# A decoder layer with a top-2 mixture of experts: one token table loaded whole, the late norms' passes moved apart, and two blocks' statistics on the scalar engine

## The chip, the cores and the metric

One core of one Trainium2 chip runs the whole program in one launch. The metric is the device time of that core in microseconds (us). The engines are TensorE (PE, with its weight loads as PEld), VectorE (DVE), ScalarE (ACT), GpSimd (POOL) and SyncE (SP); ACT, POOL and SP also issue DMAs, shown as ACTq, POOLq and SPq. Each engine runs its own instructions strictly in order.

## The reference, cut to what matters

One layer over 2048 tokens of width 1024. A mixer with attention and a recurrence comes first and is not touched. Then:

```
x = layer_norm(ALPHA * x + mix @ w_out, ln1_g, ln1_b)
scores = sigmoid(x @ w_router); sel = scores + router_bias      # 16 experts in 4 groups
best = argmax over groups of the sum of the two largest sel     # one group per token
idx  = the two experts of that group with the largest sel;  w = their scores, normalised
y[token] += w * (silu(x @ w_gate[e]) * (x @ w_up[e])) @ w_down[e]   # for its two experts
out = layer_norm(ALPHA * x + y, ln2_g, ln2_b)
```

## The kernel before, in words

Three stages follow each other: attention and recurrence to about 720 us, the out projection with router (`outproj_phase`) to about 940 us, and the experts (`moe_phase`) to the end. Tile pools make the dependences; a scheduler sets the order on DVE, ACT, POOL and SP by a simulated timeline, while PE keeps the written order. `issue_after` (through `after`) gives the scheduler an order, `hold` adds a real wait.

**Router.** For each of 16 blocks of 128 tokens `route_block` picks two experts per token on DVE, and `rank_block` gives each choice a rank within its expert and scatters the pair (token, weight) with a POOL DMA into row `expert * 2304 + rank` of table `T[j]`, one table for each of the two choices (L1238). Both tables are filled with a large number beforehand, so that the minimum of the two is the list of an expert's tokens.

**Hand-over.** `plan_slots` sorts the experts by count; slot s takes the s-th largest, with room for `CAPS[s]` tokens (336 down to 256). `fetch` reads the rows of slot 0's expert from both tables with two SP DMAs (L1499), takes the minimum and gathers the tokens' rows of x (`xg`, L1490) with three POOL DMAs. `fetch_all` reads the first 384 rows of all 16 experts from both tables with six ACT DMAs (L1515) and builds the lists of all slots on DVE (L1516 to L1529). PE multiplies dummy matrices (L77) from the moment that `early` (L1768) exists, then transposes the gathered tokens (L1542); ACT and DVE split each transposed tile into a high and a low part (L1544).

**One expert.** `gemm1` makes four pairs of products j = 0 to 3 (gate and up, L63), each of 24 matmuls per product over weights that were loaded (L1620) and split by ACT (L1628) and DVE (L1629). DVE multiplies silu(gate) by up (`sl`, L1639), ACT and DVE split the result (`h`, L1650 and L1651). Down weights are split by L1605 and L1606. `gemm2` (L1687) multiplies h with them, and between its steps PE transposes the next expert's tokens. The result is added to `zd` in memory by a POOL DMA (L1724). The weight loads of product j = 1 of slot 0 are held until slot 0's gather has landed.

**Norms.** The second layer norm is done block by block when all of a block's tokens are ready, by the table `READY`: slots 9, 11, 13 and 14 and 15 normalise two blocks each, slots 10 and 12 one. `scale` takes the statistics on DVE (L1571, L1573, L1580) and the root on POOL (L1581), `write` makes two passes of 1024 columns on DVE (L1585, L1586), and `put` scatters the rows to the output (L1591). Blocks for the next slot are fetched by `bring` (L1562). In slot 15 the last three fetched blocks and the two row tiles of its own result are normalised with `late=True`: there the root is taken on ACT as Ln and Exp (L1577, L1578).

Of the kernel before, what the change touches and what calls it, by code (L numbers as in the profile page):

```python
# [23 lines left out]
D = 1024  # L24
# [637 lines left out]
def hgrn_phase(c):  # L662

    nc, tc, a = c.nc, c.tc, c.a
    with ExitStack() as es:
# [239 lines left out]
        for g in range(NG + 1):  # L905
            if 2 <= g < 4:
                load = fill_tables(c, pad, g - 2)
                hold(c, load, c.level)
# [110 lines left out]
EROWS = 2304  # L1019
BIG = 4096.0  # L1020
NE = 16
CAPS = (336, 320, 304, 296, 288, 280, 280, 272, 264, 264, 256, 256, 256, 256, 256, 256)
# [3 lines left out]
def outproj_phase(c):  # L1026

    nc, tc, a = c.nc, c.tc, c.a
    with ExitStack() as es:
# [40 lines left out]
        c.idx = c.cp.tile([128, S // 128, 2], F32, name="idx")  # L1070

# [98 lines left out]
def route_block(c, sm, ps_r, pr, blk, rb, code, tok):  # L1170
# [11 lines left out]
    mxp, mnp = T([4, 2], "mxp"), T([4, 2], "mnp")  # L1182
    tt(mxp, sel[:, :, 0:2], sel[:, :, 2:4], OP.max)
    tt(mnp, sel[:, :, 0:2], sel[:, :, 2:4], OP.min)
    m1, m2, m3 = T([4], "m1"), T([4], "m2"), T([4], "m3")
    tt(m1, mxp[:, :, 0], mxp[:, :, 1], OP.max)
    tt(m2, mxp[:, :, 0], mxp[:, :, 1], OP.min)
    tt(m3, mnp[:, :, 0], mnp[:, :, 1], OP.max)
    tt(m2, m2, m3, OP.max)
    tt(m1, m1, m2, OP.add)  # L1190
    gm = T([1], "gm")
    v.tensor_reduce(out=gm, in_=m1, axis=AX.X, op=OP.max)
# [25 lines left out]
    return row, idx, oh, ohs  # L1218


def rank_block(c, sm, ps_r, tri, row, idx, oh, ohs):
# [14 lines left out]
    v.scalar_tensor_tensor(dst, idx, float(EROWS), rank, op0=OP.mult, op1=OP.add)  # L1236
    for j in range(2):
        nc.gpsimd.indirect_dma_start(out=c.T[j][:, :], out_offset=bass.IndirectOffsetOnAxis(ap=dst[:, j:j + 1], axis=0),  # L1238
                                     in_=row[:, j], in_offset=None)


def plan_slots(c, pl, ps):
# [9 lines left out]
    r.lt = T([NE, NE], "lt")  # L1252
# [122 lines left out]
def plan_over(c, pl, r, big):  # L1375
# [68 lines left out]
    v.scalar_tensor_tensor(orow, oe, float(EROWS), orow, op0=OP.mult, op1=OP.add)  # L1444
    yield
    c.orow = cp.tile([128, NOV], I32, name="orow")
    v.tensor_scalar(c.orow, orow, 0.0, float(NE * EROWS - 128), op0=OP.max, op1=OP.min)
# [3 lines left out]
def moe_phase(c):  # L1451
# [4 lines left out]
    with ExitStack() as es:  # L1456
# [37 lines left out]
        def fetch(row, C):  # L1494

            nch = (C + 127) // 128
            tab = sm.tile([128, 2, NCH, 2], F32, name="tab", bufs=2)[:, :, :nch]
            for j in range(2):
                nc.sync.dma_start(tab[:, j], c.T[j][ds(row, nch * 128), :].rearrange("(n p) w -> p n w", p=128))  # L1499
            tb = sm.tile([128, NCH, 2], F32, name="tb", bufs=2)[:, :nch]  # L1500
            v.tensor_tensor(out=tb, in0=tab[:, 0], in1=tab[:, 1], op=OP.min)
            ig = sm.tile([128, NCH], I32, name="ig", bufs=2)[:, :nch]
            v.tensor_scalar(ig, tb[:, :, 0], float(S - 1), None, op0=OP.min)
            io = sm.tile([128, NCH], I32, name="io", bufs=2)[:, :nch]
            v.tensor_copy(io, tb[:, :, 0])
            return gathered(dict(ig=lambda n: ig[:, n:n + 1], io=lambda n: io[:, n:n + 1], w2=lambda n: tb[:, n, 1:2]), C)

        def fetch_all(eos, big):

            both = [yp.tile([128, D], F32, name="zt", bufs=ZT)[:, :NE * NCH * 2].rearrange("p (e n w) -> p e n w", e=NE, w=2)  # L1510
                    for j in range(2)]
            for j in range(2):
# [96 lines left out]
        def gemm1(f, e, C, first=False, late=False, beside=lambda j: None):  # L1609
# [6 lines left out]
            for j in range(4):  # L1616
                ps = []
                for w in (wg, wu):
# [6 lines left out]
                    with ExitStack() as order:  # L1625
                        if j and first:
                            after(order, *f["last"])
# [133 lines left out]
        with tc.manual_schedule(engines={mybir.EngineType.PE}):  # L1761
# [12 lines left out]
            for s in range(NE):  # L1774
# [14 lines left out]
                with ExitStack() as order:  # L1789
# [6 lines left out]
                    else:  # L1796
                        after(order, f["mul"])
                        for _ in range(15):
                            next(over, None)
# [93 lines left out]
```

## Time and profile before

| what | before |
|---|---|
| median of three runs (lowest, highest) | 1678.7 us (1671.63, 1680.99) |
| the profiled execution, its span | 1675.53 us, 1674.0 us |
| busy PE, PEld, DVE, ACT, POOL | 1522.5, 1361.2, 1186.1, 816.8, 548.3 us |
| granted TensorE clock over the span | 0.969 |
| PE busy in 924 to 966 us and 966 to 1008 us | 14.31 and 30.58 of 42 us |
| PE busy in 1092 to 1386 us | 42.00 of each 42 us |

The span counts from the first to the last instruction; 1.5 us of the execution lie around it. A timeline row reads: start, duration, engine, line, operation, written tile <- read tiles, shapes, count, and in brackets how long the engine stood idle before it and for what. Rows with the same line and operation that follow closely are merged into one.

### The profile page before, as it was taken

The page shows a single profiled execution, that of the slowest core. Times are in us where ns is not written, and L with a number is a line of the kernel's source. Part 1 is how long each engine was busy: PE and PEld are TensorE (multiplying, and loading weights), DVE is VectorE, ACT ScalarE, POOL GpSimd, SP SyncE. Part 2 cuts the span into 40 slices and gives each one's busy share as a digit, 9 for nine tenths or more (in the row PEclk, how much of TensorE's full clock was granted, in tenths as well). Part 3 has the DMA queues.
Part 4 walks back from the last instruction along what each step waited for, and adds up shares of the span by engine and source line. Part 5 has one row for each costly group of instructions (what it writes and reads, how often), then busy time and mean ns, then how long its engine had stood idle before and what let it go on. Part 6 is the DMA issues. An engine that isn't in the chain of part 4 may idle for free. (4 is left out here: it accounts for less than half of the span.)

```text
span 1674.0 us, 28474 instructions
## 1 busy us (share of the span) xinstructions
PE 1522.5 (91%) x10293; PEld 1361.2 (81%) x10293; DVE 1186.1 (71%) x2780; ACT 816.8 (49%) x1824; POOL 548.3 (33%) x729
## 2 busy tenths in 40 slices
PE   8899999978898998899999379999999999999994
PEld 7899999877788887777777268988888888989883
DVE  5688888896977778777888454555555556666767
ACT  4566767676243343443342143555555555545443
POOL 3233333466644433322333211111111124232342
PEclk9999999999999999999999689999999999999997
DMA  9422222342222122263431587777777778888872
GB/s 273 154 95 89 96 96 96 121 145 75 64 64 65 58 63 60 80 233 129 175 139 77 123 225 212 195 196 199 189 202 198 204 223 247 251 246 258 248 220 100
DMA packets 241581, 258.67 MB, mean 155 GB/s; under 512 B 26224, under 2 KB 191249, under 8 KB 241436
## 3 DMA queue, kind: packets, MB, share of 16 engines
q1 hardware_dynamic: 203216, 182.03, 34.8%
q0 software_dynamic: 21088, 69.86, 15.5%
q10 hardware_dynamic: 17132, 4.91, 1.4%
q8 instruction: 83, 1.36, 0.3%
q14 instruction: 62, 0.51, 0.1%
HBM read 189.32 MB, written 69.01 MB: 154 GB/s over the span
## 5 line engine op out<-in xcount | busy, mean ns | idle before, releaser
L63 PE MATMUL ph<-xt,w 128*128 128x256 f32 (+8 forms) x3072 | 399.0, 291 | 5.7 <-DVE w L1629 5.7
L63 PEld LDWEIGHTS ph<-xt,w 128*128 128x128 f32 x3072 | 396.8, 189 | 8.8 <-DVE w L1629 7.0
L63 PE MATMUL pj<-xt,w 128*128 128x256 f32 x2016 | 290.4, 287 | 10.4 <-DVE xt L139 4.0
L63 PEld LDWEIGHTS pj<-xt,w 128*128 128x128 f32 x2016 | 259.3, 191 | 16.7 <-DVE xt L139 5.4
L1687 PE MATMUL py<-w,h 128*128 128x512 f32 (+8 forms) x936 | 243.3, 405 | 13.1 <-DVE h L1651 12.1
L1629 DVE TENSOR_TENSOR w<-raw,w 128x1024 fp32r<-128x1024 f32 x128 | 153.1, 1219 | 85.8 <-ACT w L1628 85.7
L1687 PEld LDWEIGHTS py<-w,h 128*128 128x128 f32 (+8 forms) x936 | 160.6, 179 | 58.4 <-DVE h L1651 14.7
L63 PE MATMUL py<-w,xt 128*128 128x512 f32 x672 | 174.5, 408 | 0.6 <-ACT xt L943 0.4
L1628 ACT ACTIVATE w<-raw 128x1024 fp32r<-128x1024 f32 x128 | 132.2, 1053 | 63.0 <-PE ph L63 42.5
L1724 POOL DMA_INDIRECT zd<-z,ioall x37 | 57.4, 1551 | 321.3 <-ACT xt L1544 213.7
L63 PEld LDWEIGHTS py<-w,xt 128*128 128x128 f32 x672 | 123.7, 192 | 29.0 <-issue 4.6
L1544 DVE TENSOR_TENSOR xt<-tr,xt 128x512 fp32r<-128x512 f32 (+8 forms) x84 | 50.2, 598 | 123.4 <-ACT xt L1544 123.3
L63 PE MATMUL pj<-w,xt 128*128 128x512 f32 x336 | 90.5, 409 | 0.0
L795 DVE TENSOR_TENSOR qb<-qq,F 64x256 f32<-64x256 f32 x112 | 83.1, 742 | 5.1 <-ACT F L769 2.0
L339 POOL TENSOR_SCALAR prob<-prob,den 128x128 f32<-128x128 f32 x128 | 46.2, 380 | 107.6 <-ACT prob L382 57.8
L813 DVE COPY_PREDICATED A<-mask,pl 128x512 f32<-128x512 uint8 x56 | 49.9, 891 | 40.4 <-PE pl L811 39.9
L1544 ACT ACTIVATE xt<-tr 128x512 fp32r<-128x512 f32 (+8 forms) x84 | 43.8, 521 | 70.7 <-PE tr L1542 70.5
L1634 ACT ACTIVATE sl<-ph 128x256 f32<-128x256 f32 (+8 forms) x64 | 25.7, 402 | 102.7 <-PE ph L63 102.6
L1606 DVE TENSOR_TENSOR w<-raw,w 128x2048 fp32r<-128x2048 f32 x32 | 73.1, 2284 | 0.0
L1238 POOL DMA_INDIRECT T<-row,dst x32 | 34.3, 1073 | 111.3 <-DVE dst L1236 95.2
L811 PEld LDWEIGHTS pl<-qb,kb 128*128 128x128 f32 x384 | 49.1, 195 | 26.4 <-POOL kb L799 12.7
L63 PEld LDWEIGHTS pj<-w,xt 128*128 128x128 f32 x336 | 61.6, 194 | 10.9
(387 smaller groups left out, 2864.1 us busy)
## 6 DMA issues: line engine op xcount, KB each, us to landing
raw<-in_w_gate SPq DMA_DIRECT2D x64, 512.0 KB, 5.1
raw<-in_w_up SPq DMA_DIRECT2D x64, 512.0 KB, 5.8
raw<-in_w_down SPq DMA_DIRECT2D x32, 1024.0 KB, 8.6
xd<-xt SPq DMA_DIRECT2D x32, 512.0 KB, 7.0
xr<-in_x SPq DMA_DIRECT2D x14, 1024.0 KB, 6.3
xt<-xd POOLq DMA_DIRECT2D x20, 512.0 KB, 4.8
raw<-mixT SPq DMA_DIRECT2D x16, 512.0 KB, 5.1
x1d<-x SPq DMA_DIRECT2D x16, 512.0 KB, 2.6
```

Source lines behind the costliest of these rows:

```text
L63: nc.tensor.matmul(ps, lhsT=a, rhs=b, start=i == 0, stop=i == len(steps) - 1)
L339: nc.gpsimd.tensor_scalar(prob[:, h], prob[:, h], den[:, h:h + 1], 1.0, op0=OP.mult, op1=OP.mult)
L795: nc.vector.tensor_tensor(out=qb[l][rw, :, :, o].rearrange("p a c (n i) -> p (a c) n i", i=h), in0=sec(Qv), in1=sec(Fv), op=OP.mult)
L811: nc.tensor.matmul(pl[:, ch, p], lhsT=kt[:, p, ch * 128:(ch + 1) * 128], rhs=qb[l][:, p, ch].rearrange("p o i -> p (o i)"), start=True, st ...
L813: c.level = nc.vector.copy_predicated(A.rearrange("p c h (n u i) -> p (c h n) u i", u=2, i=h)[:, :, 1], mask[:, l].rearrange("p m (n i) -> ...
L1238: nc.gpsimd.indirect_dma_start(out=c.T[j][:, :], out_offset=bass.IndirectOffsetOnAxis(ap=dst[:, j:j + 1], axis=0), in_=row[:, j], in_offse ...
L1544: f["last"] = nc.scalar.activation(hi, pt, AF.Copy), v.tensor_tensor(out=lo, in0=pt, in1=f32(hi), op=OP.subtract)
L1606: v.tensor_tensor(out=t[:, 1], in0=raw, in1=f32(t[:, 0]), op=OP.subtract)
L1628: nc.scalar.activation(t[:, 0], raw, AF.Copy)
L1629: v.tensor_tensor(out=t[:, 1], in0=raw, in1=f32(t[:, 0]), op=OP.subtract)
L1687: nc.tensor.matmul(pys[hf][:m], lhsT=lhs, rhs=rhs, start=k == 0 and i == 0, stop=k == 3 and i == len(steps[k]) - 1)
L1724: add = nc.gpsimd.indirect_dma_start(out=zv[n], out_offset=at, in_=z[:r], in_offset=None, bounds_check=S - 1, oob_is_err=False, compute_op ...
```

## The change

1. **One table.** `T[0]` and `T[1]` become one table `P`, laid out by rank: row `(rank % 128) * 272 + (rank // 128) * 16 + expert`, 272 being 17 chunks of 16 experts. Partition p then finds the first 384 ranks of all experts in 96 neighbouring numbers, and one ACT DMA loads them (L1524 of the new kernel). The row needs `rank // 128`, made by 16 comparisons and a sum (`table_row`), four DVE instructions instead of one. One fill instead of two; each scatter writes its own view of `P`.
2. **Lists in two parts.** `of_slots` builds the list of slot 0 alone from the loaded tile, and those of slots 1 to 15 after slot 0's transposes. `fetch` is left for the overflow loop, which doesn't run here.
3. **Group choice.** The sum of the two largest of four becomes the maximum over six pair sums: five DVE instructions instead of eight.
4. **Norms.** With two blocks in a slot, the first is written at product j = 1 and the second at j = 2 (both at j = 1 before). `bring` comes after the roots on POOL.
5. **Late blocks.** In slot 15 a table that has Ln and Exp is loaded once on ACT after the last silu; of the three late blocks the first keeps `scale`, the other two take their statistics on ACT (`sums_of`: a sum, a sum of squared differences, Ln, Exp).
6. `ln2_g` and `ln2_b` are loaded in the out projection (on ACT's queue) instead of in slot 0.

```diff
-    v.scalar_tensor_tensor(dst, idx, float(EROWS), rank, op0=OP.mult, op1=OP.add)
+    table_row(c, dst, rank, idx, ge, n, place, 2)
     for j in range(2):
-        nc.gpsimd.indirect_dma_start(out=c.T[j][:, :], out_offset=bass.IndirectOffsetOnAxis(ap=dst[:, j:j + 1], axis=0),
+        nc.gpsimd.indirect_dma_start(out=c.pv[2 * blk + j], out_offset=bass.IndirectOffsetOnAxis(ap=dst[:, j:j + 1], axis=0),
...
+def table_row(c, dst, rank, expert, ge, n, place, m):
+    v = c.nc.vector
+    v.tensor_tensor(out=ge, in0=rank[:, :, None].to_broadcast([128, m, NCK - 1]),
+                    in1=c.steps[:, None, :].to_broadcast([128, m, NCK - 1]), op=OP.is_ge)
+    v.scalar_tensor_tensor(place, rank, float(ROWS), expert, op0=OP.mult, op1=OP.add)
+    v.tensor_reduce(out=n, in_=ge, axis=AX.X, op=OP.add)
+    v.scalar_tensor_tensor(dst, n, float(NE - 128 * ROWS), place, op0=OP.mult, op1=OP.add)
...
-            for j in range(2):
-                rows = c.T[j].rearrange("(e r) w -> e r w", r=EROWS)[:, 0:NCH * 128].rearrange("e (n p) w -> p e n w", p=128)
-                for n in range(NCH):
-                    nc.scalar.dma_start(both[j][:, :, n], rows[:, :, n])
-            v.tensor_tensor(out=both[0], in0=both[0], in1=both[1], op=OP.min)
+            c.tabled = nc.scalar.dma_start(tab, c.P.rearrange("(p n e) w -> p n e w", p=128, n=NCK)[:, :NCH])
...
+        def sums_of(t, late):
+            z, junk = t["z"], w1p.tile([128, KC, 128], F32, name="raw1").rearrange("p k n -> p (k n)")
+            act, m = nc.scalar.activation, sm.tile([128, 4], F32, name="sums", bufs=2)
+            act(junk, z, AF.Identity, accum_out=m[:, 0:1])
+            act(m[:, 1:2], m[:, 0:1], AF.Copy, scale=-1.0 / D)
+            act(junk, z, AF.Square, bias=m[:, 1:2], accum_out=m[:, 2:3])
+            act(t["mv"][:, 0:1], m[:, 0:1], AF.Copy, scale=1.0 / D)
+            act(t["rs"], m[:, 2:3], AF.Ln, scale=1.0 / D, bias=eps2)
+            act(t["rs"], t["rs"], AF.Exp, scale=-0.5)
...
+            tab, hot = tables(r.eos)
+            slots = of_slots(tab, hot, 0, 1, big)
             f = start(0)
...
-                    if j == 1:
-                        for t in brought:
+                    if j in (1, 2):
+                        for t in brought[:1] if j == 1 else brought[1:]:
                             f["passed"] = write(t, t["z"])
...
                     if s == 0:
-                        slots = fetch_all(r.eos, big)
+                        after(order, *f["last"])
+                        slots = of_slots(tab, hot, 1, NE - 1, big)
                         nxt = start(1)
...
-                        after(order, f["low"])
+                        after(order, f["low"], f["silu"])
+                        nc.scalar.preload_act_table_set("natural_log_exp_and_others")
+                        for n, t in enumerate(brought):
+                            (sums_of if n else scale)(t, late=True)
```

PE's order is unchanged from the first instruction to the last. Three places move on the other engines.

On ACT at the hand-over, before. `zt<-T` are the six loads of `fetch_all`, `early` is what PE's dummy products wait for, `w` the split weights of slot 0's first two products, `xt` its transposed tokens:

```order
L1287 ACTIVATE eos<-py 128x16
L1515 DMA zt<-T_89 128x16x2 x3
L1515 DMA zt<-T_90 128x16x2 x2
L1768 ACTIVATE early<-tb 128x128
L1515 DMA zt<-T_90 128x16x2
L1628 ACTIVATE w_11542<-raw_11540 128x1024
L1628 ACTIVATE w_11572<-raw_11570 128x1024
L1544 ACTIVATE xt_11484<-tr 128x4x128 x2
```

The same place on ACT in the changed kernel (`tab` is the one load of `P`):

```order
L1299 ACTIVATE eos<-py 128x16
L1524 DMA tab<-P 128x96
L1655 ACTIVATE w_11581<-raw_11579 128x1024
L1655 ACTIVATE w_11611<-raw_11609 128x1024
L1797 ACTIVATE early<-tb_11484 128x128
L1558 ACTIVATE xt_11523<-tr 128x4x128 x2
```

Six loads became one, and `early` went behind the two weight casts. On DVE before, at the same place, the lists of all slots (L1516 to L1529) stood between the weights of slot 0 and its transposed tokens `xt`:

```order
L1629 TENSOR_TENSOR w_11572<-raw_11570,w_11572 128x1024
L1516 TENSOR_TENSOR zt<-zt 128x96
L1523 TENSOR_TENSOR zt<-zt,m 128x768 x2
L1525 TENSOR_REDUCE tball<-zt 128x48 x2
L1544 TENSOR_TENSOR xt_11484<-tr,xt_11484 128x4x128
L1527 TENSOR_SCALAR igall<-tball 128x48
L1529 CAST ioall<-tball 128x48
```

The same place on DVE now, from the second weight split on:

```order
L1656 TENSOR_TENSOR w_11611<-raw_11609,w_11611 128x1024
L1558 TENSOR_TENSOR xt_11523<-tr,xt_11523 128x4x128 x2
L1558 TENSOR_TENSOR xt_11523<-tr,xt_11523 128x4x80
L1558 TENSOR_TENSOR xt_11524<-tr,xt_11524 128x4x128 x2
L1558 TENSOR_TENSOR xt_11524<-tr,xt_11524 128x4x80
L1537 TENSOR_TENSOR zt<-tab,hot 128x720 x2
```

The lists of slots 1 to 15 (`128x720`) moved behind the tokens. On DVE in slot 14, from the first block's second pass (`zt<-zt,rs,b`) to `h` of product 2, before. Ahead of these rows stand `sl` of product 1, the first passes (two before, one now), a down split and two weight splits:

```order
L1586 SCALAR_TENSOR_TENSOR zt<-zt,rs,b_11383 128x1024
L1651 TENSOR_TENSOR h<-sl,h 128x256
L1586 SCALAR_TENSOR_TENSOR zt<-zt,rs,b_11383 128x1024
L1639 TENSOR_TENSOR sl<-sl,ph 128x256
L1606 TENSOR_TENSOR w_17829<-raw_17827,w_17829 128x2048
L1629 TENSOR_TENSOR w_18001<-raw_17999,w_18001 128x1024
L1629 TENSOR_TENSOR w_18031<-raw_18029,w_18031 128x1024
L1629 TENSOR_TENSOR w_18082<-raw_18080,w_18082 128x1024
L1651 TENSOR_TENSOR h<-sl,h 128x256
```

The same stretch of DVE now:

```order
L1613 SCALAR_TENSOR_TENSOR zt<-zt,rs,b_11416 128x1024
L1678 TENSOR_TENSOR h<-sl,h 128x256
L1666 TENSOR_TENSOR sl<-sl,ph 128x256
L1612 SCALAR_TENSOR_TENSOR zt<-zt,mv,g_11415 128x1024
L1633 TENSOR_TENSOR w_17864<-raw_17862,w_17864 128x2048
L1656 TENSOR_TENSOR w_18036<-raw_18034,w_18036 128x1024
L1656 TENSOR_TENSOR w_18066<-raw_18064,w_18066 128x1024
L1656 TENSOR_TENSOR w_18117<-raw_18115,w_18117 128x1024
L1613 SCALAR_TENSOR_TENSOR zt<-zt,rs,b_11416 128x1024
L1678 TENSOR_TENSOR h<-sl,h 128x256
```

The second block's two passes went behind the second `sl`; from `sl` of product 1 to `h` of product 2 both orders hold the same instructions. On ACT in slot 15 of the changed kernel, from the last silu on (before, the two `h` followed the silu at once, then five times a table load, Ln, a table load, Exp):

```order
L1661 ACTIVATE sl<-ph 128x256
L1840 ACT_TABLE_LOAD
L1601 ACTIVATE raw_18347,sums<-zt 128x1024
L1677 ACTIVATE h<-sl 128x256
L1601 ACTIVATE raw_18357,sums<-zt 128x1024
L1602 ACTIVATE sums<-sums 128x1 x2
L1603 ACTIVATE raw_18347,sums<-zt,sums 128x1024
L1603 ACTIVATE raw_18357,sums<-zt,sums 128x1024
L1677 ACTIVATE h<-sl 128x256
```

The table load and the four passes over two late blocks stand ahead of the last two `h`, or between them; the ten table loads are gone.

## Rows read from the trace of the kernel before

**Rows 1.** Busy time by stretch: stretch, its length, then PE, PEld, DVE, ACT, POOL busy us with counts, the granted TensorE clock, the DMA share and GB/s. The out projection, the hand-over, slot 0.
```profile
840.00:882.00 42.00, 42.00 (x242) 33.27 (x241) 36.55 (x145) 15.24 (x32) 14.76 (x14) 1.00 0.38 139
924.00:966.00 42.00, 14.31 (x97) 7.47 (x95) 18.63 (x105) 8.08 (x20) 10.46 (x11) 0.67 0.58 115
966.00:1008.00 42.00, 30.58 (x180) 29.34 (x181) 24.48 (x29) 17.34 (x21) 6.62 (x6) 0.86 0.77 221
```

**Rows 2.** The timeline of the hand-over, 941 to 964 us.
```profile
941.54 0.96 POOL L1238 DMA_INDIRECT T<-row,dst  x1 [0.30 <-issue]
...
943.15 1.29 SPq L1499 DMA_DIRECT2D tab<-T  x2
943.15 15.42 ACTq L1515 DMA_DIRECT2D zt<-T  x5
944.67 0.37 SPq L1620 DMA_DIRECT2D raw<-in_w_gate  x1
...
949.32 1.00 POOL L1490 DMA_INDIRECT xg<-x1d,ig  x1 [6.81 <-issue]
...
958.62 0.31 ACT L1768 ACTIVATE early<-tb 128x128 bf16<-128x128 f32 x1 [16.74 <-DMA zt<-T]
...
958.99 4.19 PE L77 MATMUL py<-ones,early 128*128 128x512 bf16 x12 [17.50 <-ACT early L1768]
...
963.02 0.60 PE L1542 MATMUL tr<-ident,xg 128*128 128x128 f32 x4
```

**Rows 3.** The timeline from there to the end of slot 0's first products.
```profile
968.07 0.26 DVE L1516 TENSOR_TENSOR zt<-zt 128x96 f32<-128x96 f32 x1 [4.63 <-DMA zt<-T]
968.36 2.98 DVE L1523 TENSOR_TENSOR zt<-zt,m 128x768 f32<-128x768 f32 x2
...
973.72 0.80 PE L1542 MATMUL tr<-ident,xg 80*128 80x80 f32 x4 [9.23 <-DVE xt L1544]
...
977.90 23.39 PE L63 MATMUL ph<-xt,w 128*128 128x336 f32 x146
...
1004.98 8.89 PE L63 MATMUL ph<-xt,w 128*128 128x336 f32 x46 [3.70 <-DVE w L1629]
...
1013.71 1.55 PE L1687 MATMUL py<-w,h 128*128 128x512 f32 x6
```

**Rows 4.** Busy time by stretch (columns as in rows 1), two stretches of 4 us in slot 0's first products.
```profile
976.00:980.00 4.00, 4.00 (x21) 3.50 (x20) 2.39 (x4) 2.95 (x5) 3.04 (x4) 0.63 0.87 285
984.00:988.00 4.00, 4.00 (x28) 4.00 (x27) 2.36 (x3) 1.43 (x2) 0.00 (x0) 1.00 1.04 377
```

**Rows 5.** DMA issues around the hand-over with KB each and us from issue to landing: slot 0's gather and table load; then the landing of all gathers into `xg` in the program; then slot 0's first gate weights.
```profile
xg<-x1d,ig POOLq DMA_INDIRECT x3, 7.1
tab<-T SPq DMA_DIRECT2D x2, 3.0 KB, 3.6
...
DMA to landing us min/median/max: 4.2/6.6/9.9
...
raw<-in_w_gate SPq DMA_DIRECT2D x1, 512.0 KB, 5.2
```

**Rows 6.** The timeline of the slot with two blocks that begins its products at 1574.8 us, from `sl` of product 1 on.
```profile
1586.44 0.42 DVE L1639 TENSOR_TENSOR sl<-sl,ph 128x256 f32<-128x256 f32 x1 [1.10 <-PE ph L63]
1586.78 2.48 DVE L1585 SCALAR_TENSOR_TENSOR zt<-zt,mv,g 128x1024 f32<-128x1024 f32 x2
...
1592.64 5.71 PE L63 MATMUL ph<-xt,w 128*128 128x256 f32 x46 [0.40 <-DVE w L1629]
...
1595.17 1.28 DVE L1586 SCALAR_TENSOR_TENSOR zt<-zt,rs,b 128x1024 f32<-128x1024 f32 x1
...
1596.70 2.28 DVE L1606 TENSOR_TENSOR w<-raw,w 128x2048 fp32r<-128x2048 f32 x1
...
1598.90 3.49 DVE L1629 TENSOR_TENSOR w<-raw,w 128x1024 fp32r<-128x1024 f32 x3
...
1602.31 0.42 DVE L1651 TENSOR_TENSOR h<-sl,h 128x256 fp32r<-128x256 f32 x1
...
1602.78 0.50 PE L1687 MATMUL py<-w,h 128*128 128x512 f32 x1 [2.58 <-DVE h L1651]
```

**Rows 7.** The timeline of slot 15's end on ACT and DVE.
```profile
1636.19 0.38 ACT L1634 ACTIVATE sl<-ph 128x256 f32<-128x256 f32 x1 [4.09 <-PE ph L63]
...
1640.79 0.43 DVE L1651 TENSOR_TENSOR h<-sl,h 128x256 fp32r<-128x256 f32 x1 [0.48 <-ACT h L1650]
1641.14 3.65 DVE L1571 BATCH_NORM_STATS2 st<-zt 128x6 f32<-128x512 f32 x6
...
1644.97 1.28 ACT L1577 ACT_TABLE_LOAD   x1 [4.21 <-DVE mv L1573]
...
1646.27 0.29 ACT L1577 ACTIVATE rs<-mv,eps 128x1 f32<-128x1 f32 x1
...
1661.63 1.28 DVE L1586 SCALAR_TENSOR_TENSOR z<-z,rs,b 128x1024 f32<-128x1024 f32 x1 [0.56 <-ACTq L1821]
```

**Rows 8.** Groups of ACT instructions by line: count, busy us, mean ns: a pass over 1024 columns, and the read of an accumulator.
```profile
L1628 ACT ACTIVATE w<-raw 128x1024 fp32r<-128x1024 f32 x128 | 132.2, 1053 | 63.0 <-PE ph L63 42.5 <-DMA raw<-in_w_up 9.5 <-DMA raw<-in_w_gate 9.4
...
L382 ACT ACTIVATION_READ_ACCUMULATOR prob<-lg,nmx 128x1 f32 x128 | 23.9, 187 | 0.0
```

**Rows 9.** One row of the out projection's timeline: the sum of scores and bias in the group choice (128x16), beside a POOL instruction of 1.02 us that began 0.19 us before it.
```profile
865.97 0.87 DVE L1174 TENSOR_TENSOR sel<-sc,rb 128x16 f32<-128x16 f32 x1
```

More of the change, by code (lines that the diff above doesn't have):

```diff
@@ L1508, in fetch_all, with fetch @@
[L1508 to L1512, printed above, removed]
-                rows = c.T[j].rearrange("(e r) w -> e r w", r=EROWS)[:, 0:NCH * 128].rearrange("e (n p) w -> p e n w", p=128)
-                for n in range(NCH):
-                    nc.scalar.dma_start(both[j][:, :, n], rows[:, :, n])
-            v.tensor_tensor(out=both[0], in0=both[0], in1=both[1], op=OP.min)
-            hot = pl.tile([128, NE, NE], F32, name="m")
+        def fetch(i):
+            at = sm.tile([128, 1], I32, name="at", bufs=1)
+            nc.sync.dma_start(at, c.over[:, ds(i, 1)])
+            tb = sm.tile([128, 2], F32, name="tb", bufs=1)
+            nc.gpsimd.indirect_dma_start(out=tb, out_offset=None, in_=c.P[:, :], in_offset=indirect(at))
+            ig = sm.tile([128, 1], I32, name="ig", bufs=1)
+            v.tensor_scalar(ig, tb[:, 0:1], float(S - 1), None, op0=OP.min)
+            io = sm.tile([128, 1], I32, name="io", bufs=1)
+            v.tensor_copy(io, tb[:, 0:1])
+            return gathered(dict(ig=lambda n: ig, io=lambda n: io, w2=lambda n: tb[:, 1:2]), 128)
@@ L1625, in gemm1 @@
                     with ExitStack() as order:
-                        if j and first:
-                            after(order, *f["last"])
+                        if first:
+                            after(order, *(f["last"] if j else (c.tabled, c.listed)))
                         nc.scalar.activation(t[:, 0], raw, AF.Copy)
@@ L1790, in moe_phase @@
                     if s == 0:
[L1791 removed]
+                        after(order, *f["last"])
+                        slots = of_slots(tab, hot, 1, NE - 1, big)
                         nxt = start(1)
[L1793 to L1795 removed]
                     else:
                         after(order, f["mul"])
+                        if s == 2:
+                            nc.scalar.dma_start(g2, a["ln2_g"].to_broadcast([128, D]))
+                            nc.scalar.dma_start(b2, a["ln2_b"].to_broadcast([128, D]))
                         for _ in range(15):
@@ L1858, in build @@
         c.z = c.dram.tile([S, D], F32, name="zd")
-        c.T = [c.dram.tile([NE * EROWS, 2], F32, name=f"T{j}") for j in range(2)]
+        c.P = c.dram.tile([128 * ROWS, 2], F32, name="P")
+        c.over = c.dram.tile([128, NOV], I32, name="over")
+        c.steps = c.cp.tile([128, NCK - 1], F32, name="steps")
+        c.nc.gpsimd.iota(c.steps, pattern=[[128, NCK - 1]], base=128, channel_multiplier=0, allow_small_or_imprecise_dtypes=True)
         with tc.tile_pool(name="w", bufs=1, reuse_waits="tile") as wp, \
```

101 lines of the change are left out of this document (48 added, 53 removed).

## The prediction

> **What bounds the kernel now.** I read the stretches first, then the timeline where PE is not busy, then what the waiting instruction stood behind on its engine. In the out projection PE is busy all 42.00 of 42 us at full clock, DVE 36.55 [rows 1]: a few small DVE instructions more or less are hidden there. In the hand-over PE is busy 14.31 of 42 us, in slot 0 30.58, at a mean granted clock of 0.67 and 0.86 [rows 1]. That is the only large hole.
>
> Its timeline names the cause. ACT needs 15.42 us to issue five of the six loads of `fetch_all`; only then, at 958.62, it runs `early`, for which PE had stood 17.50 us [rows 2]. PE's dummy products take 4.19 us, transposes begin at 963.02. Then DVE waits 4.63 us for the same loads and works on the lists of all slots, and PE stands 9.23 us for a token tile behind them on DVE [rows 3]. The products start at 977.90 and end at 1013.71, with a wait of 3.70 us [rows 3]. A second, smaller place is the slot with two norms: PE waits 0.40 us for a split weight and 2.58 us for `h` of product 2 [rows 6]. The third is the end, where DVE works from 1641.14 until the last pass at 1661.63, with 0.56 us of waiting, for ACT [rows 7].
>
> **The hand-over, step by step.** The last scatter starts at 941.54; the two table loads of before went out in 1.29 us from 943.15, the second thus near 944.0 [rows 2], when both tables had landed. The one load of now, on ACT, waits for the same scatters: 944.0. Landing 3.6 us as the old table load [rows 5]: 947.6. Before, 1.7 us passed from there to the first gather at 949.32, with three small DVE instructions. Now there are six; a minimum over 96 numbers took 0.26 us [rows 3], so 0.8 more: 950.1. Three gather issues of 1.0 us with 0.3 between them [rows 2]: the third starts at 952.7. Its landing took 7.1 us in the median while the six loads ran beside it; all gathers of the program have 6.6, from 4.2 to 9.9 [rows 5]. I take 6.6: landed at 959.3.
>
> `early` now stands behind two weight casts. The gate weights went out at 944.67, behind the table loads on SP; without these (1.29 us) at 943.4, landing 5.2 us later [rows 2, 5], up weights 0.6 us behind (an estimate; an issue takes 0.37); two casts of 1.05 us [rows 8] end near 951.4, `early` 0.3 later, dummy products to 956. So the gather is what is late next, not the casts. After its landing four of the six transpose steps are left; before, four steps took from 973.72 to 977.90 [rows 3], 1.05 us each: the products start at 963.5 instead of 977.9, a gain of 14.4 us.
>
> Slot 0's products took 35.8 us (977.90 to 1013.71). At full clock 28 matmuls go in 4 us, so 192 take 27.4; in the first stretch, at a clock of 0.63, only 21 went [rows 4]. The loss of 8.4 is 3.7 of waiting and 4.7 of low clock. The wait: DVE's order now has the weights of product 3 earlier, before the down weights, so I let it go. New cover to test: weights of product 1 are held until the gather lands (959.3), land 5.2 later, and pass ACT (1.05) near 965.6. On DVE the tokens' low parts end near 963.5, then stand two list products (2.98 for both [rows 3]) and the split of 1.2: 967.7. PE wants them at 963.5 + 6.9 = 970.4. They are in time by 2.7 us. The clock: the second pause is gone, but PE still idles before 951, so half the low-clock loss stays, 2.4. Products 29.8, a gain of 6.0. Together 20.4 us. Bounds: gather at 4.2 and no clock loss, 20.4 + 2.4 + 2.4 = 25.2; gather at 9.9, and wait and low clock both stay, 14.4 - 3.3 = 11.1.
>
> **The norms' passes.** In slot 14 DVE is never idle from `sl` at 1586.44 to `h` at 1602.31, and PE's 2.58 us end with that `h` [rows 6]. Between the two the old and the new order hold the same instructions: two first passes (2.48), two second (1.28 each), two down splits (2.28 each), five weight splits (three take 3.49), one `h`, one `sl`. What only changes places among them cannot bring the last one forward. The weight split that PE waited 0.40 us for has one pass less before it and comes in time; PE then stands those 0.40 us longer at `h`. Gain 0, in slots 11, 13 and 14. In slot 9 `h` of product 2 passes ahead of one pass and one split, but `h` of product 3 is behind them; I take 0 there too. Slots 10 and 12 have one block. Bounds: all of four slots' waits, 4 x 2.98 = 11.9 us gained; or, since `bring` now stands behind the roots on POOL, a block that lands late: its loads have most of a slot as cover, and without it PE would stand once as long as now, 2.98 lost.
>
> **The end.** ACT's last silu ends at 1636.57, now 0.4 us earlier since slot 15's own wait of that size goes. Then a table load 1.28 [rows 7], four passes over 1024 columns with an accumulator read, 4 x 1.24 [rows 8], two small copies (0.4, an estimate), and among them both `h` casts (0.42 each): the second ends at 1643.6, DVE's part of it 0.43 later, 1644.05 instead of about 1641.2. The statistics thus start 2.9 us later. They lose four of the six first passes (3.65 for six [rows 7], so 2.4) and two aggregations (about 0.3, an estimate), and the wait of 0.56 goes with the ten table loads: 3.3. Net gain 0.4. The table loads themselves ran beside DVE and are worth nothing more. Bounds: 3.3 gained if the last `h` were not held; 2.9 lost if what DVE is spared comes back as waits for ACT.
>
> The Trainium skill weighs against this part: "ScalarE: Activation LUTs", section What ACT_TABLE_LOAD costs, gives about 1.28 us for the load and 1.38 more for a drain at each change of set. In the trace the load at 1644.97 ends at 1646.25 and Ln starts at 1646.27 [rows 7], so no drain shows. By the page `h` would come 1.38 us later, the end would lose 1.0, and the sum would be 1656; I go by the row.
>
> **The rest at nothing.** The group choice loses three DVE instructions and the rank gains three, per block; PE covers both. One table fill less lies long ahead of its use. `ln2_g` and `ln2_b` move to a stage with a DMA share of 0.38 [rows 1].
>
> **The sum.** The profiled execution took 1675.53 us, span and 1.5 us around it, 3.2 below the median of the runs and inside them. 1675.5 - 20.4 - 0.4 = 1654.7, so 1655.
>
> **Rivals.** *The spread pays in full*, as the waits at `h` seem to promise [rows 6]: 11.9 us more, 1643. Against it stands the same sum of DVE work.
> *A thin hand-over*: the table's load shares the queue engines with 1 MB of weights and lands late, the gather takes 9.9, product 1's weights, held by it, come late: the bound of 11.1, 1664. For it: the median landing of 7.1 in that place [rows 5].
> *The change doesn't do what it says*: the hole is set by another thing (eslot, the gather), and slot 0 starts when it did: 1675. Against it: both PE waits end with the loads that go.
> *DVE overruns the out projection*, the one on the other side. DVE has 5.45 us of slack per 42 [rows 1], 1.7 per block of about 13 us. A small instruction that met a POOL instruction took 0.87 us [rows 9]. If all nine of a block's choice and rank did, instead of about 0.2, that is 6 us, 4.3 over the slack, 60 in 14 blocks: 1655 + 60 = 1715. It decides from 1.5 us per block over the slack, where it eats the 20.8. The Trainium skill, "SBUF — State Buffer", section Who interferes with whom, says that a DVE instruction with two SBUF inputs contends with a GpSimd one that reads SBUF, and that a reduction never does. By that rule the new order, with reductions for some of the two-input maxima, meets POOL less and this rival falls away; row 9 agrees with its first half, no row here shows the second.
>
> **How the numbers follow.** Forecast 0.62, full spread 0.10, thin hand-over 0.18, no effect 0.07, overrun 0.03. A difference of 0.5%, 8.4 us, is what a measurement tells from none. Faster: 0.62 + 0.10 + 0.18 = 0.90; same 0.07; slower 0.03. The forecast's own range is 1649 to 1662 (the hand-over's bounds narrowed by a third, as both ends need two things at once); the 8-in-10 range adds most of the thin hand-over and part of the spread: 1646 to 1666.
>
> **What would show it.** Right: one table load landing near 948, gathers near 950, transposes from about 957, slot 0's products from about 963.5 without a wait over 1 us, DVE's list products (720 columns) after the tokens; in slots 9, 11, 13 and 14 PE still waits about 3 us for `h`; at the end DVE stands some 3 us for the last `h`, and one table load. Wrong: products of slot 0 later than 968 (gather or table), PE waits in those slots gone (the spread works), PE under 42.00 in the out projection (overrun).

## The result, and the profile after

The changed kernel takes 1658.53 us in the median of 4 runs (1657.11 to 1661.63), the kernel before 1675.86 (1671.63 to 1680.99): a ratio of 0.990, with a 95% interval from 0.986 to 0.993. It is faster, as forecast, inside the range of 1646 to 1666 and 3.5 us above the forecast of 1655. The profiled execution took 1661.63 us, the longest of the four, with a span of 1660.1. One of the four executions of pad_both, below, took 1865.01 us at a granted clock of 0.746; the time given for it there is the median of the other three.

Where the time went is read best by cutting both spans at the same events. The rows of before that mark the cuts and were not shown yet (first product of the out projection, first products of slots 1, 9 and 15, last put):

```profile
732.35 0.73 PE L63 MATMUL py<-w,xt 128*128 128x512 f32 x2 [0.40 <-ACT xt L943]
...
1033.24 2.94 PE L63 MATMUL ph<-xt,w 128*128 128x320 f32 x19
...
1378.36 17.84 PE L63 MATMUL ph<-xt,w 128*128 128x264 f32 x146
...
1615.48 17.41 PE L63 MATMUL ph<-xt,w 128*128 128x256 f32 x146
...
1663.19 0.99 POOL L1737 DMA_INDIRECT out<-z,ioall  x1 [1.25 <-DVEq L1821]
```

and the same events of the changed kernel, with its last scatter and slot 0's first products:

```profile
737.84 11.80 PE L63 MATMUL py<-w,xt 128*128 128x512 f32 x48 [0.54 <-ACT xt L943]
...
944.19 0.97 POOL L1240 DMA_INDIRECT P<-row,dst  x1 [0.30 <-issue]
...
964.90 26.61 PE L63 MATMUL ph<-xt,w 128*128 128x336 f32 x170
...
1017.43 28.22 PE L63 MATMUL ph<-xt,w 128*128 128x320 f32 x192
...
1362.27 23.65 PE L63 MATMUL ph<-xt,w 128*128 128x264 f32 x192
...
1601.87 22.88 PE L63 MATMUL ph<-xt,w 128*128 128x256 f32 x192
...
1648.36 0.98 POOL L1764 DMA_INDIRECT out<-z,io  x1 [0.80 <-DVEq L1856]
```

| stretch, us | before | after | change | forecast |
|---|---|---|---|---|
| start to the out projection | 732.35 | 737.84 | +5.5 | 0 |
| out projection, to the last scatter | 209.19 | 206.35 | -2.8 | 0 |
| last scatter to slot 0's products | 36.36 | 20.71 | -15.7 | -14.4 |
| slot 0 | 55.34 | 52.53 | -2.8 | -6.0 |
| slots 1 to 8 | 345.12 | 344.84 | -0.3 | 0 |
| slots 9 to 14 | 237.12 | 239.60 | +2.5 | 0 |
| slot 15, to the last put | 47.71 | 46.49 | -1.2 | -0.4 |
| last put to the end | 10.81 | 11.74 | +0.9 | 0 |
| span | 1674.0 | 1660.1 | -13.9 | -20.8 |

In the stage of the first line the change leaves out one of the two table fills (a DMA) and makes one small constant; the rest is as before. In the twelve profiles of this study the out projection starts between 732.4 and 737.8 us: from 732.35 to 736.77 in the three kernels with two fills, from 732.85 to 737.84 in the nine with one. So the 5.5 us lie within what executions of either kind differ by, and can't be put down to the change.

Busy time by stretch, in the stretches of [rows 1], columns as there:

```profile
840.00:882.00 42.00, 42.00 (x240) 32.97 (x239) 37.47 (x143) 15.67 (x34) 14.44 (x14) 1.00 0.37 139
924.00:966.00 42.00, 23.55 (x139) 14.13 (x138) 24.76 (x132) 11.09 (x26) 10.21 (x11) 0.72 0.52 161
966.00:1008.00 42.00, 39.40 (x239) 36.76 (x238) 24.86 (x30) 20.64 (x27) 8.00 (x7) 1.00 1.02 307
```

PE stays at 42.00 in the out projection, is busy 23.55 us instead of 14.31 in the hand-over and 39.40 instead of 30.58 in slot 0, where the mean granted clock is now 1.00. The hand-over's timeline answers to [rows 2] and [rows 3]:

```profile
948.00 0.33 ACTq L1524 DMA_DIRECT2D tab<-P  x1
...
950.78 0.33 DVE L1537 TENSOR_TENSOR zt<-tab,hot 128x48 f32<-128x48 f32 x2 [6.53 <-DMA tab<-P]
...
951.51 0.29 ACT L1797 ACTIVATE early<-tb 128x128 bf16<-128x128 f32 x1
...
951.86 5.30 PE L77 MATMUL py<-ones,early 128*128 128x512 bf16 x12 [8.39 <-ACT early L1797]
952.22 1.28 POOL L1505 DMA_INDIRECT xg<-x1d,ig  x1 [7.06 <-issue]
...
955.07 0.91 POOL L1505 DMA_INDIRECT xg<-x1d,ig  x1 [0.30 <-issue]
...
959.94 0.66 PE L1556 MATMUL tr<-ident,xg 128*128 128x128 f32 x4 [1.93 <-DMA xg<-x1d,ig]
...
961.00 0.77 PE L1556 MATMUL tr<-ident,xg 80*128 80x80 f32 x4 [0.18 <-DMA xg<-x1d,ig]
...
966.07 1.72 DVE L1537 TENSOR_TENSOR zt<-tab,hot 128x720 f32<-128x720 f32 x2
```

One load, issued at 948.00, is used on DVE from 950.78; `early` runs at 951.51, behind the second weight cast, as the lists of slot 0 end; the first gather is issued at 952.22; PE waits 1.93 us for a landed gather and for nothing longer until the products start; the list products over 720 columns stand behind the tokens. PE's wait for `early` is 8.39 us instead of 17.50, and the 9.23 us behind the lists are gone.

### The profile page after: what moved, and what is told of

It reads as the page before. It is cut to its first block, busy times and chain, and to the rows that moved or that the text cites. A ratio compares the mean times of both kernels' runs of the same rounds, so it can differ in the third digit from the quotient of the medians.

```text
span 1660.1 us, 28463 instructions
## 1 busy us (share of the span) xinstructions
PE 1526.8 (92%) x10293; PEld 1360.7 (82%) x10293; DVE 1187.5 (72%) x2779; ACT 809.9 (49%) x1827; POOL 525.5 (32%) x732
## 5 line engine op out<-in xcount | busy, mean ns | idle before, releaser
L1751 POOL DMA_INDIRECT zd<-z,io x40 | 62.0, 1551 | 329.8 <-ACT xt L1558 206.2
L63 PE MATMUL pj<-w,xt 128*128 128x512 f32 x336 | 91.7, 413 | 0.0
L1633 DVE TENSOR_TENSOR w<-raw,w 128x2048 fp32r<-128x2048 f32 x32 | 73.2, 2286 | 0.0
L1729 ACT ACTIVATE z<-py,tb 128x512 f32<-128x512 f32 (+1 forms) x62 | 42.7, 689 | 61.1 <-PE py L1714 59.6
L811 PEld LDWEIGHTS pl<-qb,kb 128*128 128x128 f32 x384 | 49.2, 195 | 26.5 <-issue 12.5
```

The source lines that it names most:

```text
L63: nc.tensor.matmul(ps, lhsT=a, rhs=b, start=i == 0, stop=i == len(steps) - 1)
L811: nc.tensor.matmul(pl[:, ch, p], lhsT=kt[:, p, ch * 128:(ch + 1) * 128], rhs=qb[l][:, p, ch].rearrange("p o i -> p (o i)"), start=True, st ...
L1633: v.tensor_tensor(out=t[:, 1], in0=raw, in1=f32(t[:, 0]), op=OP.subtract)
L1729: nc.scalar.activation(z[:r, hs], py[:r], AF.Copy, scale=weight)
L1751: add = nc.gpsimd.indirect_dma_start(out=zv[n], out_offset=at, in_=z[:r], in_offset=None, bounds_check=S - 1, oob_is_err=False, compute_op ...
```

## Experiments

All ran beside the kernel before, which took 1672.8 to 1673.3 us in the median there. The changed kernel was not run again beside them. pad_x, below, does its work with some tiles at other addresses and took 1654.55 us, so a distance of some 4 us from 1658.5 says nothing by itself; the stages of the profiles are compared instead.

**The parts alone.** Three runs take one part of the diff each, in its own hunks. hand_only is the changed kernel with the old `beside`, `bring` and end put back:

```diff
-                    if j in (1, 2):
-                        for t in brought[:1] if j == 1 else brought[1:]:
+                    if j == 1:
+                        for t in brought:
...
-                    after(order, *(t["root"] for t in brought))
...
-                            (sums_of if n else scale)(t, late=True)
+                            scale(t, late=True)
```

> The hand-over alone (one table by rank, lists in two parts), with both norm passes beside product 1, bring without a wait and the old statistics at the end. Theory (nearly all of the gain is the hand-over): about 1659 us, the same as the whole change within 3 us; the products of slot 0 start about 21 us after the last scatter was issued (36.4 before, 20.7 in the changed kernel); PE's waits in the two-block slots are the old 0.40 for a weight and 2.6 for h; the end from the start of slot 15's products to the last put takes the old 47.7 us. Rival (the three parts share the gain): 1664 us or more, so at least 5 us slower than the whole change.

Measured: 1657.29 us, ratio 0.991 (0.989 to 0.9925). Two rows of its timeline, slot 0's first products and the wait for `h` in slot 11:

```profile
964.06 2.21 PE L63 MATMUL ph<-xt,w 128*128 128x336 f32 x12
...
1466.52 0.50 PE L1714 MATMUL py<-w,h 128*128 128x512 f32 x1 [2.58 <-DVE h L1678]
```

The last scatter was issued at 942.94, so the products start 21.1 us behind it; the old wait of 2.58 us for `h` is back; slot 15 to the last put takes 47.8 us. The hand-over alone gives 15.4 us of gain (12.5 to 18.4) and the whole change's time: the theory holds, the rival is out.

spread_only is before with the hunks in `beside` and `bring` alone.

> The kernel before with only the passes spread over products 1 and 2 and the wait of bring for the roots. Theory (the same DVE work stands between sl of product 1 and h of product 2): within 3 us of the kernel before; PE's 0.40 us for a weight split goes in slots 9, 11, 13 and 14 and comes back at h, 3.0 to 3.3 us instead of 2.6. Rival 1 (the spread pays): PE's waits for h fall under 1 us, 8 to 12 us faster. Rival 2 (the longer wait costs twice, by a low clock behind it): 3 us slower.

Measured: 1673.26 us, ratio 1.000 (0.999 to 1.002).

```profile
1482.68 0.50 PE L1687 MATMUL py<-w,h 128*128 128x512 f32 x1 [3.25 <-DVE h L1651]
```

The weight wait of 0.40 us is gone and the wait for `h` is 3.25 us, where [rows 6] has 2.58. Slots 9 to 14 take 237.0 us, against 237.1 before. Rival 1 is out; rival 2 is not seen here. In the changed kernel's own profile it is, in slots 11 and 13, where nine products took 4.19 us behind the wait, against 2.33 in slot 14:

```profile
1548.93 0.80 PE L1714 MATMUL py<-w,h 128*128 128x512 f32 x1 [3.31 <-DVE h L1678]
...
1550.23 4.19 PE L1714 MATMUL py<-w,h 128*128 128x512 f32 x9
```

one_list, with the same order in these slots, takes 239.9 us there too, but pad_both, end_h and pad_x, also with waits of 3.25 us, take 236.5 to 236.9. So the longer wait costs up to 2.8 us in some executions and nothing in others.

end_only is before with `sums_of` and the new block under `if last`.

> The kernel before with only the end changed: statistics of two of the three late blocks on ACT, one table load. Theory: 0.4 to 1.2 us faster than before, not to be told by the time; DVE stands 2 to 3 us for the last h and starts its statistics later by as much, and the end from the start of slot 15's products to the last put takes 46.5 us instead of 47.7. Rival (ACT becomes the bound at the end): 1.5 us or more longer, 49 us. Rival 2 (ten table loads were on the path): 44 us or less.

Measured: 1671.94 us, ratio 0.999 (0.998 to 1.000), not to be told by the time. The end takes 46.65 us (1613.58 to 1660.23), as the theory said, and both rivals are out.

**The order on DVE.** The two-block slots keep their waits; is that DVE's time or its order? In `h_both` the splits of the next slot's first weights and the second block's passes (`beside(4)`, at product 2 in the changed kernel) are tied behind the low part of `h` of product 3:

```diff
+                        if j < 2 and lows:
+                            after(order, lows[-1])
                         v.tensor_tensor(out=t[:, 1], in0=raw, ...
...
+                if j == 3:
+                    lows[:] = [low] if f.get("two") else []
+                    with ExitStack() as order:
+                        after(order, low)
+                        beside(4)
```

> The changed kernel with DVE's order altered in the two-block slots: the four splits of the next slot's first weights and the second block's two passes stand behind the low parts of h of products 2 and 3. Theory (PE waits for h only because of what stands ahead of it on DVE, and that could stand behind): PE's waits for h in slots 9, 11, 13 and 14 (12.3 us in the changed kernel) fall under 1 us each, about 10 us faster than the changed kernel, 1648 us. Rival (DVE is short in these slots as a whole): the wait moves to the low parts of the next slot's tokens or to its weights, and the time stays within 3 us of 1658.

Measured: 1648.23 us, ratio 0.985 (0.9825 to 0.988). The waits for `h` in these slots are gone, as the theory said. Slots 9 to 14 take 231.6 us, 5 to 8 less than in the profiles with the changed kernel's order (236.5 to 239.9), so of the 10 us by the times not all can be put down to the order. And the rival has a part of the truth:

```profile
1535.76 4.63 DVE L1658 TENSOR_TENSOR w<-raw,w 128x1024 fp32r<-128x1024 f32 x4
...
1540.30 0.69 DVE L1558 TENSOR_TENSOR xt<-tr,xt 128x512 fp32r<-128x512 f32 x1
...
1541.04 0.66 PE L1556 MATMUL tr<-ident,xg 128*128 128x128 f32 x4 [2.82 <-DVE xt L1558]
```

Now four weight splits in a row (4.63 us) stand ahead of the low part of a token tile, and PE waits 2.82 us for it. `h_tokens` ties each of the four splits behind one token tile instead:

```diff
-                            after(order, lows[-1])
+                            after(order, lows[-1], f["split"][2 * j + len(ps)])
```

> h of products 2 and 3 first on DVE in the two-block slots, as in the run before, and each of the next slot's four weight splits behind the low part of one of the next slot's four token tiles. Theory (in the run before the wait had moved to the token tiles because five DVE instructions stood ahead of their low parts, not because DVE lacks time): the three waits of 2.05, 2.82 and 2.83 us for the low parts fall under 1 us each, slots 9 to 14 take 225 us instead of 231.6, and the time is about 1642 us. Rival (DVE as a whole is the bound in these slots): the waits move again, to the weights of the next slot, and slots 9 to 14 stay within 2 us of 231.6, 1648 us.

Measured: 1641.92 us, ratio 0.982 (0.978 to 0.986). The waits for tokens are gone and slots 9 to 14 take 223.1 us (1356.59 to 1579.68). One wait moved: in slot 12, which has one block, PE stands 1.41 us for a cast of `h` on ACT, and the slot takes 39.7 us instead of 36.7. At the end 3.9 us are given back (50.4 us instead of 46.5), which no theory had said:

```profile
1604.48 1.06 ACT L1602 ACTIVATE raw<-zt 128x1024 f32<-128x1024 f32 x1 [3.04 <-DMA zt<-zd,fin]
...
1605.99 4.43 PE L1723 MATMUL py<-w,h 128*128 128x512 f32 x18 [2.04 <-ACT h L1680]
```

Slot 15 comes sooner, ACT stands 3.04 us for the load of a late block, and the cast of `h` that PE waits for stands behind ACT's statistics.

**The split list.** `one_list` makes the lists of all slots ahead of the first gather:

```diff
-            slots = of_slots(tab, hot, 0, 1, big)
+            slots = of_slots(tab, hot, 0, NE, big)
```

> The changed kernel with the lists of all slots made at once ahead of the first gather. Theory: the one load is what the hand-over gains by, the split list a smaller part: the 768-column products, reductions and conversions (about 4 us instead of 0.8) stand before the first gather, slot 0's products start 3 to 4 us later from the last scatter (24 instead of 20.7), the time is 3 us longer, 1661. Rival (the gather is not what slot 0 waits for): no difference, 1658. Rival 2 (the lists behind the tokens cost slot 0 its wait for h of product 2): slot 0 gains 2 us back and the difference is 1 us.

Measured: 1659.69 us, ratio 0.992 (0.988 to 0.995); the profile decides.

```profile
943.85 0.97 POOL L1240 DMA_INDIRECT P<-row,dst  x1 [0.30 <-issue]
...
968.08 1.12 PE L63 MATMUL ph<-xt,w 128*128 128x336 f32 x5
```

Slot 0's products start 24.2 us behind the last scatter, 3.5 later. Slot 0 then takes 49.3 us, without a wait for `h`, instead of 49.4 to 52.5 with the split list. So of the 15.7 us that the hand-over gained 3.5 are the split list's, of which slot 0 can give back up to 3. The other 12 or so are the one load's together with what moved with it (`early` behind the weight casts above all); no run parts these. The theory and rival 2 are both right in part.

**The held h at the end.** `end_h` puts ACT's statistics behind the last cast of `h`:

```diff
-                        after(order, f["low"], f["silu"])
+                        after(order, f["low"], f["high"])
```

> The changed kernel with the table load and the four ACT passes of the end behind the last h cast, so that the last h is not held. Theory (the end gained only 1.2 us because DVE stood 2.25 us for that h): DVE's wait goes, the end from the start of slot 15's products to the last put takes 44.3 to 45 us instead of 46.5. Rival (what DVE is spared comes back as a wait for ACT's statistics, which now end 2 us later): 46 us or more. By the time alone not to be told from the changed kernel.

Measured: 1652.65 us, ratio 0.989 (0.986 to 0.992), but the end takes 46.57 us (1590.78 to 1637.35): the rival's number.

```profile
1616.12 0.43 DVE L1678 TENSOR_TENSOR h<-sl,h 128x256 fp32r<-128x256 f32 x1 [0.48 <-ACT h L1677]
...
1634.89 1.28 DVE L1613 SCALAR_TENSOR_TENSOR z<-z,rs,b 128x1024 f32<-128x1024 f32 x1
1635.95 1.09 POOL L1764 DMA_INDIRECT out<-z,io  x1 [3.16 <-DMA out<-zt,fin]
1637.35 0.98 POOL L1764 DMA_INDIRECT out<-z,io  x1 [0.30 <-POOLq L1856]
```

DVE waits 0.48 us for the last `h` instead of 2.25 and its last pass starts 44.1 us into the slot instead of 44.9. The rival's mechanism isn't it either: DVE never waits for ACT's statistics. It waits 0.80 us for a product of PE, and then the first of the two last puts is held until the puts of the late blocks have landed (3.16 us, DMA), the second behind it. These are what is late next. That the whole run is 6 us shorter than the changed kernel is not the end's doing: in its profile the out projection starts at 732.85 us, slot 0 takes 49.4 us and slots 9 to 14 236.9, other executions' lengths of stages that this edit leaves alone.

**Where the operands stand.** At the full granted clock a block of the out projection takes 13.17 us in every kernel so far with the new table and 13.04 in the others, with PE never idle. The change moves SBUF addresses: the weights there stand 128 bytes lower, the token tiles 768 higher. `pad_both` has the edit below; `pad_x` has 24 for the 16 and the old `steps`. Both have the token tiles at one address. They differ by 128 bytes in that of the weights, with which most other tiles of the stage move (PE's results as DVE stores them, the router's small tiles):

```diff
-        c.steps = c.cp.tile([128, NCK - 1], F32, name="steps")
+        c.steps = c.cp.tile([128, NCK + 31], F32, name="steps")[:, :NCK - 1]
...
-    ge, n, place = T([2, NCK - 1], "ge"), T([2], "nrank"), T([2], "place")
+    ge, n, place = T([2, NCK - 1], "ge"), T([2], "nrank"), T([16], "place")[:, :2]
```

> The changed kernel with 128 bytes per partition of padding in the constants and 128 in the router's small tiles: the out projection's weights stand at the very SBUF addresses of the kernel before again, its token tiles 1024 bytes behind theirs. Theory A (a product's duration hangs on where its operands stand): the 512-column products of the out projection take 389 ns in the median again instead of 393, a block 13.04 us instead of 13.17, and from the first to the last scatter 161.3 instead of 163.5 us: about 2 us faster than the changed kernel, 1656.5. Theory B (the new rank and choice on DVE and POOL slow PE by using the same memory): 393 ns and 13.17 us stay, the time as the changed kernel's.

> The changed kernel with padding in the router's small tiles alone: the token tiles of the out projection stand 1024 bytes behind those of the kernel before, the weights stay 128 bytes ahead of theirs. If the address of the stationary operand or of what DVE and POOL write there decides: 389 ns and 13.04 us per block; if that of the weights, which stream, decides: 393 ns and 13.17 us.

Measured: 1654.78 us, ratio 0.990 (0.986 to 0.994), and 1654.55, 0.990 (0.9865 to 0.994); the times don't tell them apart. The products of the out projection from 800 to 920 us (count, then least, median and longest ns), in end_only, the changed kernel, pad_both and pad_x:

```profile
L63 PE MATMUL py<-w,xt x445: 387/389/496, 799.8 to 919.9; 128*128 128x512 f32 x149
```
```profile
L63 PE MATMUL py<-w,xt x439: 390/393/500, 799.8 to 919.9; 128*128 128x512 f32 x147
```
```profile
L63 PE MATMUL py<-w,xt x445: 387/390/496, 799.6 to 919.9; 128*128 128x512 f32 x149
```
```profile
L63 PE MATMUL py<-w,xt x440: 390/393/500, 799.8 to 920.0; 128*128 128x512 f32 x147
```

With the weights 128 bytes higher, where they were, a block takes 13.06 us again; with the token tiles moved alone 13.17. Theory A holds for the product and the block: of the operands that PE reads in these products, only the weights stand at other addresses in the two kernels. It does not hold for the whole stage in this execution (163.8 us from the first to the last scatter, not 161.3). There the granted clock fell in an early block, behind a wait of 1.78 us for DVE:

```profile
774.00:778.00 4.00, 4.00 (x16) 3.15 (x15) 2.60 (x31) 0.16 (x1) 1.07 (x1) 0.71 0.54 214
```

`best`, below, has the same addresses and the same wait with the clock at 1.00 behind it, and needs 162.2 us between these scatters, where the seven profiles with the changed kernel's weight addresses need 163.5 to 163.6: the gain there is 1.3 us.

**Together.** `best` joins h_tokens, in slots 9 to 14, single-block ones too, with the end of end_h and the addresses of pad_both.

> All that helped together: h of products 2 and 3 first in slots 9 to 14 with each weight split behind a token tile, slot 15 in the order of the changed kernel with ACT's statistics behind the last h cast, and the out projection's weights at the addresses of the kernel before. Theory (the gains stand in different stages and add up): slots 9 to 14 223 us (239.6 in the changed kernel), the end 45 to 46.5, out projection blocks 13.06 us: 1637 us. Rival (the end gives it back, since the late blocks are read from what slot 14 wrote and their loads land no sooner): the end takes 50 us as in the run before, 1641.

Measured: 1636.57 us, ratio 0.978 (0.976 to 0.981). Slots 9 to 14 take 218.3 us (1358.42 to 1576.69), the end 46.57, a block of the out projection 13.06. In the middle of the late slots, beside the changed kernel's:

```profile
1443.00:1563.00 120.00, 112.58 (x766) 103.48 (x765) 76.47 (x96) 57.53 (x79) 26.14 (x25) 0.94 0.88 254
```
```profile
1436.00:1541.00 105.00, 105.00 (x754) 97.85 (x753) 76.50 (x96) 57.17 (x77) 31.48 (x25) 1.00 0.95 279
```

PE is busy all of 105 us, with DVE at 76.50: DVE was never short of time there.

## Why the prediction was right, and where its terms were off

**The hand-over** came near the forecast: 15.7 us in the profile, 15.2 in hand_only, 14.4 forecast. The stretch takes 33.7 to 36.4 us in the profiles with the old hand-over, 19.5 to 21.1 in the eight with the new one and the split list. The chain was right, but single terms were off and made up for each other, which is luck. The table's load went out later behind the last scatter than I had it (3.8 us against 2.5); its data was used 2.8 us after that (3.6), and the first gather followed 1.4 us later (2.5). So the first gather (8.0 us behind that scatter; forecast 8.6) and the third (10.9; 11.2) were still sooner, and the casts ahead of `early` cost nothing. The thin hand-over is out: PE has the third gather's tile at 961.00, 5.9 us after its issue, where I took 6.6.

**Slot 0's products** took 30.6 us, 29.8 forecast. The term that was mis-sized is what the slot as a whole gives, 6.0 forecast and 2.8 measured: PE's 3.70 us for a weight fell to 0.49, but a wait of 2.11 us for `h` of product 2 came up behind the products, where I had looked no further:

```profile
983.91 1.06 ACT L1655 ACTIVATE w<-raw 128x1024 fp32r<-128x1024 f32 x1 [5.24 <-DMA raw<-in_w_gate]
985.00 1.23 DVE L1656 TENSOR_TENSOR w<-raw,w 128x1024 fp32r<-128x1024 f32 x1 [8.55 <-ACT w L1655]
...
999.62 0.50 PE L1714 MATMUL py<-w,h 128*128 128x512 f32 x1 [2.11 <-DVE h L1678]
```

DVE stood 8.55 us behind a weight split whose load landed late; the stretch now runs at a DMA share of 1.02. Across the profiles with this hand-over and the split list slot 0 takes 49.4 to 52.5 us and that wait is absent, 0.8, 1.5 or 2.1 us: 6.0 is its best case.

**The norms' passes.** A gain of 0 was right, and so was the way: the wait for the weight goes and comes back at `h`. Over slots 9 to 14 PE's waits for a weight, 1.6 us, are gone, and those for `h` rose from 12.1 to 13.8. Slot 14 of the changed kernel, against [rows 6]:

```profile
1585.66 3.49 DVE L1656 TENSOR_TENSOR w<-raw,w 128x1024 fp32r<-128x1024 f32 x3
...
1589.06 1.28 DVE L1613 SCALAR_TENSOR_TENSOR zt<-zt,rs,b 128x1024 f32<-128x1024 f32 x1
1590.26 0.42 DVE L1678 TENSOR_TENSOR h<-sl,h 128x256 fp32r<-128x256 f32 x1
...
1590.73 0.50 PE L1714 MATMUL py<-w,h 128*128 128x512 f32 x1 [3.25 <-DVE h L1678]
```

2.58 + 0.40 makes 2.98 of the 3.25 us. The reason given, that no order of the same work brings `h` forward, holds for the order that the change makes and no further. Three of the five weight splits (3.49 us) belong to the next slot, and h_both and h_tokens put them, and the second block's passes, behind the last `h`. What the "full spread" promised, to which I gave 0.10, was there to be had, but not by moving the passes alone.

**The end** gained 1.2 us, 0.4 forecast (bounds 3.3 and -2.9). DVE stood for the last `h` as said, 2.25 us where I had 2.9:

```profile
1622.34 1.28 ACT L1840 ACT_TABLE_LOAD   x1
...
1623.64 1.06 ACT L1601 ACTIVATE raw<-zt 128x1024 f32<-128x1024 f32 x1
...
1628.98 0.42 DVE L1678 TENSOR_TENSOR h<-sl,h 128x256 fp32r<-128x256 f32 x1 [2.25 <-ACT h L1677]
```

ACT's one table load ends at 1623.62 and the next activation starts at 1623.64: the Trainium skill's "ScalarE: Activation LUTs", section What ACT_TABLE_LOAD costs, counts 1.38 us more for a drain, and this trace again shows none. That the held `h` is what keeps the end from gaining 3.3 is refuted by end_h.

**At nothing** I put the out projection. PE stayed at 42.00 of 42 and DVE did not overrun it, so that rival is out. Its first step was nearer than I had it, though: the prediction let DVE meet POOL less in the new order, but it is busy 37.47 of 42 us instead of 36.55. `sel` (128x16, the instruction of [rows 9]) took 0.87 to 0.88 us in every block between 800 and 920 us; now it takes that in four of nine and 1.73 to 1.75 us in five, each time ending 0.04 or 0.05 us behind the same POOL pass (`x<-x,g`). PE covers it. And a block takes 0.13 us more with PE always busy, by where the weights stand, about 1.8 us over 14 blocks, a term that I did not have. The before profile hid it: its first blocks there ran at a granted clock of 0.83, and the stage took 209.2 us (spread_only, at 0.91, 206.2). end_only, at 1.00, needs 204.7 and the seven kernels with the new addresses 206.3 to 206.5.

```profile
740.00:760.00 20.00, 17.51 (x99) 13.66 (x99) 15.20 (x37) 6.85 (x15) 8.46 (x6) 0.83 0.82 310
```

The sum of 20.8 is the changed stretches' own: from the last scatter to slot 1 the three profiles with the old hand-over take 88.7 to 91.7 us, the eight with the new one and the split list 70.0 to 73.2; the forecast went by the slowest of the three. The means, 90.1 and 71.3 us, differ by 18.8, where I had 20.4; with 1.2 of the end, less the 1.8 of the out projection, that makes 18.2, where 17.3 were measured. So the forecast was 3.5 us too low mostly by the term of slot 0 (6.0, where the profiles' means of 55.1 and 50.9 us give 4.1) and by the out projection.

## What to carry to other kernels

When PE waits for a product of another engine, list what that engine does between the input's arrival and the result, and ask of each piece whose deadline is nearer; a busy engine is short of time only if all of the list is due first. A transfer that many later steps share should be one load in the layout in which it is read, and the part that the first step needs should be cut off ahead of the rest. Sum a forecast against more than one profile, or at least against stretches whose clock was undisturbed.

## What the runs showed of the hardware that was not expected

- A 512-column product of the out projection takes 389 to 390 ns in the median with its streaming weights at one SBUF address and 393 ns with them 128 bytes lower, in all twelve profiles, at a granted clock of 1.00 (800 to 920 us). Why, and whether the other tiles that moved along have a part in it, no run here shows.
- Behind a wait of 3.3 us the granted clock fell in some executions and not in others. In slot 11 of the changed kernel it is 0.50, the lower of its two levels (1.2 GHz), in the 4 us from 1470, after PE was busy 1.05 of the 4 us before. In pad_both it is 1.00, the upper level (2.4 GHz), in the 4 us from 1464, after PE was busy 0.80 of the 4 us before; there, and in end_h, slot 11 with the same wait takes 39.1 us instead of 41.9. What decides between the two, no run here shows.

```profile
1466.00:1470.00 4.00, 1.05 (x5) 0.54 (x3) 4.00 (x5) 0.66 (x1) 0.00 (x0) 0.93 1.01 366
1470.00:1474.00 4.00, 3.70 (x11) 3.04 (x12) 2.74 (x5) 1.02 (x2) 0.98 (x1) 0.50 1.00 266
```

- The last scatter's issue ended at 945.16 and the load that waits for it went out at 948.00. The Trainium skill, "Perfetto Trace Analysis", section DMA Instruction — SWDGE (GPSIMD), says that the profile's end is that of writing descriptors, and the semaphore follows the confirmed write. The 2.84 us between the two agree with that order; what they consist of, no run here shows.
